# Scaling the attention products of a pair of heads: one vector product in place of two activations

## Chip, core and metric

The kernel runs on one core of a Trainium2 chip. The metric is the device time of one execution in microseconds; the median of the runs of a kernel counts.

## What is computed

Two layers of a hybrid backbone on 256 context and 512 latent tokens of width 1024. Each layer has modulated normalisation, one input projection, three groups of heads side by side (differential attention, grouped-query attention, a bidirectional gated delta rule), an output projection, and a SwiGLU. What matters here is the attention of the first two groups:

```python
# differential: 4 heads, two score components of 32 columns each, V of 64 columns
s = jnp.einsum('bqhcd,bkhcd->bhcqk', q, k).astype(jnp.float32) * scale
p = jax.nn.softmax(s, axis=-1)
p = p[:, :, 0] - lam * p[:, :, 1]
return jnp.einsum('bhqk,bkhe->bqhe', p.astype(v.dtype), v)
# grouped-query: 6 query heads, 2 key/value heads, 64 columns
s = jnp.einsum('bqhgd,bkhd->bhgqk', qg, k).astype(jnp.float32) * dh ** -0.5
p = jax.nn.softmax(s, axis=-1)
o = jnp.einsum('bhgqk,bkhd->bqhgd', p.astype(v.dtype), v)
```

Latent queries read all 768 tokens, context queries the 256 context tokens. Context outputs are computed in the first layer alone.

## The kernel before

The ten attention heads are worked off as five pairs of heads: two pairs of differential heads (numbers 0 and 1) and three pairs of grouped-query heads (2 to 4), in the order of `HORD`. For each pair, `attention` (line 1270) calls `attend` (line 1175) once per block of 128 queries: six blocks in layer 0, four in layer 1. That makes 30 and 20 calls, 50 in all. The letters of `ASTEP` (line 51) say at which step of a pair the next block of queries runs (`a`), the next pair's operands are loaded and turned (`f`, `t`), the pair before is finished (`o`), and control goes back to the surrounding plan (`y`).

One call does the following for both heads of the pair. `scores` (line 1166) multiplies queries and keys into a PSUM tile of two banks; there are two such tiles, used in turn. `softmax` (line 1156) takes the row maximum from it on VectorE (line 1162, tile `nm`), and ScalarE writes the exponentials `P` to SBUF, with their row sums in a column of `Z` (line 1163). A grouped-query head has one component, a differential head two; for the latter, VectorE forms the factor `cR` and adds the second component to the first (lines 1188 to 1191). The reciprocal `R` of the first sum is taken for each head as soon as its softmax is written (line 1186). The unnormalised `P` is then turned by TensorE, up to three blocks of 128 columns into one PSUM bank (`pt`, line 1197), and copied to `PT` in SBUF; by `EVD` (line 47), the first of the copies of a head with one component goes to VectorE (line 1199), the others to ScalarE (line 1201). Over the kernel that is 140 softmaxes and 180 copies, 60 of them on VectorE.

After both heads come the products with V: both heads side by side into the first 128 columns of one bank (`pv`, line 1207), a copy `OTs` on ScalarE (line 1209), and a transpose into columns 128 to 255 of the same bank (line 1210). Two activations then write the 64 columns of each head to `O`, scaled by that head's `R` (lines 1211 and 1212). `O` holds the outputs of a pair for all tokens; `attn_post` (line 1237) normalises those of differential heads, turns them and passes them on.

`pt`, `pv` and the transposes of operands (`exp`, `stk`) share one ring of PSUM banks (`ring`, line 150). It has two banks, `m0` and `m1`; from the step `w0` of the plan on there are four. A bank is free again when its last reader is through. `R` and `Z` each have four buffers.

In between, the plan (`PLAN`, line 38) sets the steps of the gated delta rule (`gdn_invert`, `gdn_post`, `gdn_step`, `gdn_out`), whose matmuls, copies and vector work stand in the same queues. The plan sets the order in which work is written down; the order on each engine is then drawn up when the kernel is built, from priorities and a simulated timeline (line 1668: `schedule_with_timeline_sim=True`). The engines themselves work in order. In the profile, helpers stand for the lines that call them: L186 is any activation, L189 a copy on ScalarE, L165 a product or sum of two tensors, L183 a fused scalar and tensor operation, L192 a matmul, L195 a transpose.

Of the kernel before, what the change touches and what calls it, by code (L numbers as in the profile page):

```python
# [13 lines left out]
AF = mybir.ActivationFunctionType  # L14
ALU = mybir.AluOpType
# [64 lines left out]
class Region:  # L80
# [8 lines left out]
    def slot(self, name, dt=F32, tag="s"):  # L89
        return self.pool.tile([128, self.cols], dt, tag=tag, name=name, bufs=self.tags[tag])  # L90
# [8 lines left out]
class Net:  # L99
# [16 lines left out]
    def slot(self, name, dt=F32, tag="s"):  # L116
        return self.R.slot(name, dt, tag)

# [166 lines left out]

    def ada_rows(self, R):

        self.cb = []
        for i in range(2):
            b = R.tiny("cb", [128, 1024], bufs=2)  # L290
            self.dma(b, self.A["crow"][i:i + 1].to_broadcast([128, 1024]))
            w = self.W.slot("adaw", F32, "raw")
            self.act(w, b, AF.Tanh, scale=0.5)
            self.stt(b, w, 1.0, b, ALU.add, ALU.mult)
            self.cb.append(b)

    def ada_row(self, R, w, l, ct, src, queue):

        queue.dma_start(out=w, in_=src)
        m = self.md[l][:, ct]  # L300
        j = R.tiny("junk", [128, 1024], mybir.dt.bfloat16)
        for ci in range(2):
            self.stt(j, w, 0.5, self.cb[ci], ALU.mult, ALU.mult, accum_out=m[:, ci:ci + 1])
        self.add(m, m, self.adab[:, l, ct:ct + 1].to_broadcast([128, 2]), self.g)

    def ada_next(self):

        if self.ada_todo:
            l, ct = self.ada_todo.pop(0)
            self.ada_row(self.R, self.W.slot("adaw", F32, "raw"), l, ct, self.A["ada_t"][48 * l + ct], self.nc.scalar)  # L310

# [473 lines left out]
    def gdn_post(self, l, tt):  # L785
        Z = self.GP.slot("Z")
        self.g.memset(Z[:, :768], 0.0)
        Zv = Z[:, :768].rearrange("p (h i) -> p h i", i=64)
        w = BLK[l][[tt in g for g in GDN_GROUPS].index(True)]
# [6 lines left out]
        T = self.GP.slot("ZT")  # L796
        self.v.transpose(out=T[:, :768], in_=Z[:, :768])
        Tv = T[:, :768].rearrange("p (h i) -> p h i", i=64)
# [354 lines left out]
        self.dma(xv[:, t0:], src[:, t0:])  # L1153
        return xv

    def softmax(self, ps, nk, zi, Z):

        P = self.slot("P", tag="p")
        nm = self.tiny("nm", [128, 1], bufs=4)
        pin = ps[:, :, :384] if nk == 768 else ps  # L1160
        pout = P[:, :768].rearrange("p (a b) -> p a b", a=2) if nk == 768 else P[:, :nk]
        self.v.tensor_reduce(out=nm, in_=pin, axis=AX.XY if nk == 768 else AX.X, op=ALU.max, negate=True)  # L1162
        self.act(pout, pin, AF.Exp, bias=nm, accum_out=Z[:, zi:zi + 1])
        return P

    def scores(self, pairs, qt, nk):
# [8 lines left out]
    def attend(self, l, pair, O, qts):  # L1175

        for qt in qts:
            nk = TOK if qt >= 2 else CTX
            nkb = nk // 128
            PTs, Rs = [], []  # L1180
            for comps, V in pair:
                Z = self.tiny("Z", [128, 2], bufs=4)
                Ps = [self.softmax(self.scores(pr, qt, nk), nk, ci, Z) for ci, pr in enumerate(comps)]
                P = Ps[0]
                R = self.tiny("R", [128, 1], bufs=4)
                self.v.reciprocal(out=R, in_=Z[:, 0:1])
                if len(comps) == 2:
                    c = self.tiny("cR", [128, 1], bufs=4)
                    self.v.reciprocal(out=c, in_=Z[:, 1:2])
                    self.stt(c, c, self.lam[:, l:l + 1], Z[:, 0:1], ALU.mult, ALU.mult)  # L1190
                    self.stt(P[:, :nk], Ps[1][:, :nk], c, P[:, :nk], ALU.mult, ALU.add)
                PT = self.slot("PT", tag="q")
                for i, k0 in enumerate(range(0, nk, 384)):
                    n = min(384, nk - k0)
                    ps = self.ring("pt")
                    for k in range(0, n, 128):
                        self.tr(ps[:, k:k + 128], P[:, k0 + k:k0 + k + 128])
                    if i < EVD[l][len(comps) - 1]:
                        self.v.tensor_copy(PT[:, k0:k0 + n], ps[:, :n])
                    else:  # L1200
                        self.cp(PT[:, k0:k0 + n], ps[:, :n])
                PTs.append(PT)
                Rs.append(R)
            pv = self.ring("pv")
            for kb in range(nkb):
                for c in range(2):
                    self.mm(pv[64 * c:64 * c + 64, :128], pair[c][1][:, kb], PTs[c][:, 128 * kb:128 * kb + 128], kb == 0, kb == nkb - 1)
            OT = self.R.tiny("OTs", [128, 128], bufs=2)
            self.cp(OT, pv[:, :128])
            self.tr(pv[:, 128:256], OT)  # L1210
            for c in range(2):
                self.act(O[:, qt, 64 * c:64 * c + 64], pv[:, 128 + 64 * c:192 + 64 * c], AF.Identity, scale=Rs[c])

    def attn_prep(self, l, i):

# [457 lines left out]
```

## Time and profile before

| | |
|---|---|
| median of 3 runs | 2218.24 us (2215.98 to 2219.58) |
| profiled execution, own time | 2220.72 us |
| its span | 2218.9 us |
| mean granted clock of TensorE | 0.928 of full speed |
| instructions | 37524 |
| busy: TensorE, VectorE, ScalarE, GpSimd | 2038.1, 1371.7, 850.0, 494.0 us |

The table of busy time says how much of the span an engine works; a TensorE that is busy is not necessarily at its peak, since the ends of its matmuls are modelled. The lists of waits say which engine stood idle in front of a group of instructions, and whose instruction ended that; "issue" means that nothing in the profile shows a cause. PE is TensorE's matmul, PEld its weight load, DVE VectorE, ACT ScalarE, POOL GpSimd, SP SyncE.

### The profile page before, as it was taken

Reading aid. Unit: us, or ns where it says so; the run is one execution under the profiler, and the core shown is the slowest. Engines: PE = TensorE matmul, PEld = TensorE weight load, DVE = VectorE, ACT = ScalarE, POOL = GpSimd, SP = SyncE. Lnnn points to the kernel's source line nnn. Section 1 sums busy time; section 2 is a strip of 40 time slices with the busy share of each in tenths; the row PEclk is TensorE's granted clock in tenths of the full one; section 3 lists DMA queues with packets and bytes.
Section 4 is the critical chain, followed back from the end, with each engine's and each line's share of the span. In section 5 each row is a group of like instructions: output and inputs, shape, how many; then the busy total and the mean of one; then the engine's idle time right before and its main releaser. Section 6 shows DMA issues by size and latency. Waiting matters only on the chain. (4 is left out here: it accounts for less than half of the span.)

```text
span 2218.9 us, 37524 instructions
## 1 busy us (share of the span) xinstructions
PE 2038.1 (92%) x14786; PEld 1688.2 (76%) x14786; DVE 1371.7 (62%) x2565; ACT 850.0 (38%) x1709; POOL 494.0 (22%) x797
## 2 busy tenths in 40 slices
PE   7999968798889999999999899975898989999997
PEld 3777766575668888888888789764676688888887
DVE  6747865757645646665756576688658655444444
ACT  5434235556644321212122444222566644222223
POOL 2204487230004101000000420456212022000002
PEclk9999976797899999999999999996599999999999
DMA  8345443120152324343424312343211152322331
GB/s 297 132 158 166 147 121 79 46 66 19 40 208 82 108 85 161 106 132 100 157 95 138 130 58 66 114 128 103 53 44 53 47 184 92 108 76 98 103 104 58
DMA packets 167601, 236.51 MB, mean 107 GB/s; under 512 B 75328, under 2 KB 109248, under 8 KB 167424
## 3 DMA queue, kind: packets, MB, share of 16 engines
q10 hardware_dynamic: 46160, 144.92, 20.1%
q1 hardware_dynamic: 121264, 89.18, 13.2%
q8 instruction: 117, 1.92, 0.3%
q14 instruction: 60, 0.49, 0.1%
HBM read 198.00 MB, written 36.04 MB: 105 GB/s over the span
## 5 line engine op out<-in xcount | busy, mean ns | idle before, releaser
L189 ACT ACTIVATE whi<-raw 128x1024 fp32r<-128x1024 f32 (+4 forms) x246 | 220.9, 912 | 484.9 <-PE dps L192 196.3
L165 DVE TENSOR_TENSOR wlo<-raw,whi 128x1024 fp32r<-128x1024 f32 (+4 forms) x236 | 249.0, 1068 | 221.9 <-ACT whi L189 220.0
L192 PE MATMUL gu<-ahi,wlo 128*128 128x512 f32 x672 | 262.5, 391 | 1.1 <-DVE wlo L165 1.1
L192 PE MATMUL gu<-ahi,whi 128*128 128x512 f32 x672 | 262.2, 391 | 0.0
L192 PE MATMUL dps<-acth,whi 128*128 128x512 f32 (+1 forms) x560 | 184.3, 345 | 0.6 <-ACT acth L189 0.4
L192 PE MATMUL dps<-acth,wlo 128*128 128x512 f32 (+1 forms) x560 | 183.9, 344 | 0.0
L192 PE MATMUL gu<-alo,whi 128*128 128x512 f32 x672 | 167.0, 390 | 0.0
L183 DVE SCALAR_TENSOR_TENSOR junk<-adaw,cb 128x1024 bf16<-128x1024 f32 x112 | 136.9, 1222 | 37.2 <-DMA adaw<-ada_t 36.3
L1162 DVE TENSOR_REDUCE nm<-S 128x1 f32<-128x768 f32 (+1 forms) x140 | 117.5, 845 | 57.6 <-PE S L192 56.2
L192 PEld LDWEIGHTS gu<-ahi,wlo 128*128 128x128 f32 x672 | 126.2, 188 | 27.6 <-DVE wlo L165 1.5
L192 PE MATMUL tps<-whi,ahi 128*128 128x512 f32 (+4 forms) x368 | 136.7, 376 | 10.8 <-ACT gk L189 8.0
L192 PEld LDWEIGHTS gu<-alo,whi 128*128 128x128 f32 x672 | 126.1, 188 | 26.7
L192 PEld LDWEIGHTS gu<-ahi,whi 128*128 128x128 f32 x672 | 126.3, 188 | 25.7
L183 DVE SCALAR_TENSOR_TENSOR h<-dps,md,h 128x512 f32<-128x512 f32 (+1 forms) x128 | 80.5, 633 | 104.6 <-PE dps L192 104.4
L192 PE MATMUL tps<-wlo,ahi 128*128 128x512 f32 (+4 forms) x368 | 138.1, 376 | 2.5 <-DVE wlo L165 2.5
L192 PE MATMUL tps<-whi,alo 128*128 128x512 f32 (+4 forms) x368 | 136.4, 371 | 0.0
L165 POOL TENSOR_TENSOR sqc<-sqc 128x256 f32<-128x256 f32 x35 | 34.0, 971 | 448.2 <-ACT sqc L186 447.7
L186 ACT ACTIVATE P<-S,nm 128x768 f32<-128x768 f32 (+1 forms) x140 | 114.3, 817 | 48.8 <-DVE nm L1162 35.6
L165 POOL TENSOR_TENSOR md<-md,adab 128x2 f32<-128x2 f32 x56 | 33.0, 588 | 434.9 <-DVE junk L183 434.9
L192 PE MATMUL dps<-actl,whi 128*128 128x512 f32 (+1 forms) x560 | 123.0, 344 | 0.0
L192 PEld LDWEIGHTS dps<-acth,whi 128*128 128x128 f32 x560 | 105.2, 188 | 15.2 <-ACT acth L189 0.6
L192 PEld LDWEIGHTS dps<-acth,wlo 128*128 128x128 f32 x560 | 105.2, 188 | 14.5
(315 smaller groups left out, 4740.2 us busy)
## 6 DMA issues: line engine op xcount, KB each, us to landing
raw<-w_u ACTq DMA_DIRECT2D x88, 512.0 KB
adaw<-ada_t ACTq DMA_DIRECT2D x56, 512.0 KB
adaw<-ada_p ACTq DMA_DIRECT2D x24, 512.0 KB
raw<-w_o ACTq DMA_DIRECT2D x24, 512.0 KB
raw<-w_d ACTq DMA_DIRECT2D x44, 256.0 KB
raw<-w_d ACTq DMA_DIRECT2D x32, 320.0 KB
adaq<-ada_q SPq DMA_DIRECT2D x16, 512.0 KB
raw<-w_t ACTq DMA_DIRECT2D x16, 512.0 KB
```

Source lines behind the costliest of these rows:

```text
L165: (eng or self.v).tensor_tensor(out=out, in0=a, in1=b, op=op)
L183: self.v.scalar_tensor_tensor(out=out, in0=a, scalar=sc, in1=b, op0=op0, op1=op1, **k)
L186: self.s.activation(out=out, in_=in_, func=func, **k)
L189: self.s.activation(out=out, in_=in_, func=AF.Copy, **k)
L192: self.t.matmul(out, lhsT, rhs, start=start, stop=stop)
L1162: self.v.tensor_reduce(out=nm, in_=pin, axis=AX.XY if nk == 768 else AX.X, op=ALU.max, negate=True)
```

## The change

The row sums of both heads of a pair go into one tile `Z` of 2x2 columns. One reciprocal takes the first column of both heads, after the softmaxes, the combinations and the transposes of both are written. One product of two tensors on VectorE writes both heads' 64 columns to `O`, out of PSUM, with `R` spread over 64 columns each, in place of the two activations on ScalarE. `Z` and `R` keep four buffers each, now one per pair and not one per head.

```diff
-    def softmax(self, ps, nk, zi, Z):
+    def softmax(self, ps, nk, z):
...
-        self.act(pout, pin, AF.Exp, bias=nm, accum_out=Z[:, zi:zi + 1])
+        self.act(pout, pin, AF.Exp, bias=nm, accum_out=z)
...
-            PTs, Rs = [], []
-            for comps, V in pair:
-                Z = self.tiny("Z", [128, 2], bufs=4)
-                Ps = [self.softmax(self.scores(pr, qt, nk), nk, ci, Z) for ci, pr in enumerate(comps)]
+            PTs = []
+            Z = self.tiny("Z", [128, 2, 2], bufs=4)
+            for hd, (comps, V) in enumerate(pair):
+                Ps = [self.softmax(self.scores(pr, qt, nk), nk, Z[:, hd, ci:ci + 1]) for ci, pr in enumerate(comps)]
                 P = Ps[0]
-                R = self.tiny("R", [128, 1], bufs=4)
-                self.v.reciprocal(out=R, in_=Z[:, 0:1])
                 if len(comps) == 2:
                     c = self.tiny("cR", [128, 1], bufs=4)
-                    self.v.reciprocal(out=c, in_=Z[:, 1:2])
-                    self.stt(c, c, self.lam[:, l:l + 1], Z[:, 0:1], ALU.mult, ALU.mult)
+                    self.v.reciprocal(out=c, in_=Z[:, hd, 1:2])
+                    self.stt(c, c, self.lam[:, l:l + 1], Z[:, hd, 0:1], ALU.mult, ALU.mult)
                     self.stt(P[:, :nk], Ps[1][:, :nk], c, P[:, :nk], ALU.mult, ALU.add)
...
                 PTs.append(PT)
-                Rs.append(R)
+            R = self.tiny("R", [128, 2], bufs=4)
+            self.v.reciprocal(out=R, in_=Z[:, :, 0])
             pv = self.ring("pv")
...
             self.tr(pv[:, 128:256], OT)
-            for c in range(2):
-                self.act(O[:, qt, 64 * c:64 * c + 64], pv[:, 128 + 64 * c:192 + 64 * c], AF.Identity, scale=Rs[c])
+            self.mul(O[:, qt].rearrange("p (c d) -> p c d", c=2), pv[:, 128:256].rearrange("p (c d) -> p c d", c=2),
+                     R.unsqueeze(2).to_broadcast([128, 2, 64]))
```

## Rows read from the trace of the kernel before

**Rows 1.** The page: busy time of each engine, share of the span, instructions.
```profile
PE 2038.1 (92%) x14786; PEld 1688.2 (76%) x14786; DVE 1371.7 (62%) x2565; ACT 850.0 (38%) x1709; POOL 494.0 (22%) x797
```

**Rows 2.** Busy time by stretch, 340 to 660 plus 1560 to 1785 us.
```profile
sum 545.00, PE 476.12 PEld 358.07 DVE 346.56 ACT 326.44 POOL 105.94; mean PE 238.06 PEld 179.04 DVE 173.28 ACT 163.22 POOL 52.97
```

**Rows 3.** 1680 to 1720 us: engines' busy time, clock, DMA; then tile O on ACT.
```profile
1680.00:1720.00 40.00, 33.95 (x395) 26.73 (x391) 39.33 (x123) 25.97 (x62) 4.18 (x5) 0.88 0.13 38
...
1680.00:1720.00 40.00, 2.06 (x8) 0.88 0.13 38
```

**Rows 4.** Tile R: what its instructions waited for (us, times), whole span.
```profile
  PE pv L195: 20.7, 19
  ACT O L186: 5.1, 5
  ACT P L186: 5.0, 9
```

**Rows 5.** Groups of ACT, DVE: busy us, mean ns of one | idle before, releaser.
```profile
L186 ACT ACTIVATE O<-pv,R 128x64 f32<-128x64 f32 x100 | 25.9, 312 | 21.0 <-PE pv L195 20.7
...
L1162 DVE TENSOR_REDUCE nm<-S 128x1 f32<-128x768 f32 x112 | 106.2, 951 | 46.0 <-PE S L192 44.9
...
L1186 DVE RECIPROCAL R<-Z 128x1 f32<-128x1 f32 x100 | 14.6, 155 | 10.8 <-ACT O L186 5.1 <-ACT P L186 5.0
```

**Rows 6.** Timeline, 1739.8 to 1742.2 us: start, duration, instruction, idle before and releaser.
```profile
1741.17 0.27 PE L195 MATMUL pv<-ident,OTs 128*128 128x128 f32 x1
...
1741.37 0.96 DVE L1162 TENSOR_REDUCE nm<-S 128x1 f32<-128x768 f32 x1
1741.48 0.52 ACT L186 ACTIVATE O<-pv,R 128x64 f32<-128x64 f32 x2 [1.34 <-PE pv L195]
...
1742.05 0.33 PE L195 MATMUL pt<-ident,P 128*128 128x128 f32 x1 [0.28 <-ACT O L186]
```

**Rows 7.** PE's waits, 340 to 660 us: us in total, times, longest.
```profile
PE S L192 <- ACT P L186: 5.2, 10, 1.2
...
PE pv L192 <- ACT PT L189: 2.5, 5, 0.7
PE pt L195 <- ACT O L186: 2.4, 3, 1.6
...
PE exp L195 <- ACT O L186: 1.5, 2, 0.9
...
PE otr L195 <- ACT O L186: 0.6, 1, 0.6
```

**Rows 8.** The same for weight loads, 340 to 660 us.
```profile
PEld pt L195 <- ACT O L186: 4.2, 8, 1.8
...
PEld exp L195 <- ACT O L186: 1.9, 2, 1.1
...
PEld otr L195 <- ACT O L186: 0.8, 1, 0.8
```

**Rows 9.** Waits of PE and of its weight loads, 1560 to 1785 us.
```profile
PE S L192 <- ACT P L186: 5.6, 10, 1.9
...
PE pv L192 <- ACT PT L189: 2.4, 3, 1.4
...
PE pt L195 <- ACT O L186: 0.8, 3, 0.3
...
PEld pt L195 <- ACT O L186: 1.8, 4, 0.5
...
PEld exp L195 <- ACT O L186: 0.2, 1, 0.2
```

**Rows 10.** Products of gk (two rows) and of X on DVE: ns min/median/max, first and last start.
```profile
L165 DVE TENSOR_TENSOR gk<-gk,arskv x12: 279/280/1844, 241.0 to 1490.1; 128x128 f32<-128x128 f32 x12
L165 DVE TENSOR_TENSOR gk<-gk,arsgq x10: 547/553/560, 283.7 to 1531.8; 128x384 f32<-128x384 f32 x10
...
L165 DVE TENSOR_TENSOR X<-scan,U x44: 548/554/561, 342.2 to 1697.2; 64x384 f32<-64x384 f32 x44
```

**Rows 11.** All waits: ACT's exponentials for row maxima.
```profile
ACT P L186 <- DVE nm L1162: 35.6, 34, 4.5
```

## Prediction

> **What bounds the kernel now.** First the table of busy time: TensorE (PE) is busy 92% of the span, VectorE (DVE) 62%, ScalarE (ACT) 38% [rows 1]. The change touches attention only, so the next view is busy time by stretch. Attention runs in 340 to 660 us (layer 0) and 1560 to 1785 us (layer 1). In these 545 us PE is busy 476.1, which leaves 68.9 us idle; DVE is busy 346.6 and ACT 326.4, so 64% and 60% [rows 2]. The two helper engines are about equally loaded there: moving work from one to the other is not a move to a free engine. One stretch has another limit: from 1680 to 1720 us DVE is busy 39.3 of 40 us while ACT has 26.0, and four of the pairs of activations that the change removes lie in it [rows 3].
>
> Next, the removed work itself. The 100 activations into O take 312 ns each, 25.9 us together, and ACT stood idle 20.7 us in front of 19 of them for PE's transpose of the products [rows 4, 5]. A pair overlaps and takes 0.52 us from start to end [rows 6]. The same rows show the pattern to look for: the transpose at 1741.17, the pair at 1741.48, and PE's next transposes of P, which want a bank of PSUM, at 1742.05, idle 0.28 us with ACT's O named as releaser. While `rings` holds two banks, `pv` keeps one of them until both activations are through.
>
> Last, PE's list of waits, since only PE's idle time in these stretches is to be had. O ended 9 waits of PE's matmuls, 5.3 us together, and 16 of its weight loads, 8.9 us [rows 7 to 9]. Other work of ACT ended more: P in front of new scores 10.8 us in 20 waits, the copies PT in front of the product with V 4.9 us in 8 [rows 7, 9].
>
> **The change part by part.** *Removed from ACT:* 50 pairs at 0.52 us, 25.9 us of busy time, and their 20.7 us of idle time. *Added to DVE:* 50 products of 128x128 out of PSUM with a factor spread over 64 columns. The trace has the same shape and spread out of SBUF: gk<-gk,arskv, median 280 ns, at worst 1844. What PSUM adds I take from two products with 384 columns: 553 ns out of SBUF, 554 out of PSUM, so nothing [rows 10]. I take 0.29 us. *Reciprocals:* 100 of one column at 155 ns become 50 of two columns [rows 5]; I leave the price at 0.155 us, and a second column at double price would add 7.8 us of DVE time, hidden like the rest. DVE's balance per pair is 0.29 - 0.155 = +0.135 us, 6.8 us over 50.
>
> *On the path, the bank.* From the end of the transpose to the release of `pv`, 0.52 us become 0.29, if DVE is as free as ACT was: 0.23 us less. I count the 16 places where O ended a wait of PE's weight loads: 16 x 0.23 = -3.7 us. Ends: nothing, if each of these waits is taken over by another; and if each product stands behind a row maximum (951 ns, [rows 5]), 16 x (0.95 - 0.23) = +11.5 us. I take the first value, as the busy shares of 64% and 60% give both engines nearly the same chance of being occupied.
>
> The Trainium skill's page "Perfetto Trace Analysis", section "Optimizing Scalar/DVE Operations", speaks against this step: it puts the overhead of one operation on PSUM at some 125 ns for VectorE and 51 for ScalarE. An estimate from that page, with the clocks of 0.96 and 1.2 GHz that its page "Trainium Kernel Development and Optimization", section "NeuronCore Architecture", gives, puts 128 columns at 0.26 us and twice 64 at 0.21, and the term would be about +0.8 us in place of -3.7. The rows above disagree with it on both sides: no surcharge for PSUM on DVE, and 0.52 us for the pair.
>
> *On the path, ACT's queue.* What stands behind a removed pair comes 0.52 us sooner. ACT has 140 exponentials P and, by the code, 120 of the 180 copies PT (60 go to DVE); about one in five of these 260 has a pair right in front of it (50/260 = 0.19). Of the 28 waits of PE that P and PT ended, that makes 28 x 0.19 x 0.52 = -2.8 us. Ends: nothing, where P itself was late because its row maximum was (P waited 35.6 us for it in 34 places, [rows 11]); and all 28 shortened by a whole pair, -14.6 us.
>
> *On the path, DVE.* Where PE or ACT sets the pace, 0.135 us more on DVE are hidden under PE's matmuls; if that cover is gone everywhere they cost 6.8 us. They surely count where DVE is saturated: four pairs, 4 x 0.135 = +0.5 us. DVE also loses waits: its reciprocal R stood idle 10.8 us, 5.0 for P's sum and 5.1 for an older pair of O that still read R's buffer [rows 4, 5]. The new reciprocal is written after both heads, when the sums have long been there, and four buffers now hold four pairs of heads, not two. In its place the product itself waits for PE's transpose, on DVE, with row maxima behind it; that is the rival below. I enter both at nothing.
>
> *Buffers and DMAs:* Z and R grow to 16 and 8 bytes a row; no transfer is issued, moved or put behind a wait; SP's and POOL's queues stay as they are. The square and the transposes of O after each head group now wait for DVE, 0.23 us sooner or a row maximum later, four and fifty times; both lie inside the bounds above. The order on each engine is drawn up at build time, so neighbours may trade places anywhere in attention; the trace of before can't price that, and the bounds of the two path terms are my measure of it.
>
> Sum: -3.7 - 2.8 + 0.5 = **-6.0 us**. The profiled execution took 2220.72 us, 2.5 above the median of 2218.24, with a span of 2218.9; the removed work is the same in both, so the median becomes about 2212. About 0.2%, 4.4 us, is what a measurement of this kernel can tell from no change.
>
> **The rivals.** *Slower: DVE waits where ACT waited.* DVE works in order. If the product stands there before the transpose is done, the 20.7 us that ACT lost come to DVE, and the next row maximum is late, with it P and the scores behind it. For it: P already waits for row maxima in 34 places [rows 11], and from 1680 to 1720 us DVE has nothing to spare. Against it: 10.8 us of idle time at the reciprocals leave the same queue. Price: 20.7 - 10.8 + 6.8 (all of DVE's extra work then counts) = +16.7, less 2.8 for ACT's relief: +13.9 us, 2232. It decides once idle time in front of the product passes some 7 us (10.8 + 2.8 - 6.8). The same page and section of the Trainium skill advises moving work to ScalarE when VectorE is saturated, which is this change turned round; rows 3 bear that out for 40 of the 545 us.
>
> *No change: PE's next wait takes over.* A release that comes sooner only lets PE reach the next transposes, which need P, or scores, which need a bank that P still holds. For it: P and its row maximum end more of PE's waits than O does. Against it: 5.3 us of waits are O's alone. Time: 2218, give or take 4.
>
> *Far faster: ACT was the brake.* If all 28 waits that P and PT end shrink by a whole pair: -3.7 - 14.6 + 0.5 = -17.8 us, 2200. For it: ACT feeds both of PE's commonest waits. Against it: only one in five has a pair in front.
>
> *Not what it says:* the 50 products would have to take as long as the pairs, 0.5 us, as some of arskv's did beside POOL's work (its longest was 1844 ns). Then the bank term vanishes and the balance is about -2 us; it falls in the case of no change.
>
> **How the numbers follow.** Forecast (-12 to -1 us around -6): chance 0.48, of it 0.33 beyond 4.4 us and 0.15 within. Far faster: 0.10. No change: 0.17, of it 0.14 within 4.4 us, 0.01 above and 0.02 below. Slower: 0.25. So faster 0.33 + 0.10 + 0.02 = 0.45, same 0.15 + 0.14 = 0.29, slower 0.25 + 0.01 = 0.26. The range reaches to the far faster case, 2200, and into most of the slower one, 2230; beyond the ends lie half of the first and some of the second, under 2 in 10. The forecast's own range is 2206 to 2217.
>
> **What would show it.** Right: 50 products at 0.28 to 0.30 us; 50 reciprocals at about 0.155 with little idle time in front; waits of PE for the product below 5.3 us; ACT's busy time down by about 26 us; waits of scores for P below 10.8 us. Wrong: idle time in front of the product well over 7 us with row maxima behind it, P's waits for them above 35.6 us, attention's two stretches longer than 545 us; or a difference that lies outside attention, where nothing was changed.

## The result and the profile after

The changed kernel takes 2203.77 us (median of 4 runs, 2200.47 to 2204.93), the kernel before 2218.91 in the same session: ratio 0.993 [0.9909, 0.9951], 15.1 us less. Its profiled execution took 2204.24 us with a span of 2202.4, 16.5 less than the span before.

The change did to its own instructions what it says. The view of tile R shows duration (ns, min/median/max), first and last start, then idle time of the engine before them, by what ended it (us, times):

```profile
L1202 DVE RECIPROCAL R<-Z x50: 144/158/167, 357.8 to 1754.0; 128x2 f32<-128x2 f32 x50
L165 DVE TENSOR_TENSOR O<-pv,R x50: 268/280/292, 370.0 to 1767.1; 128x128 f32<-128x128 f32 x50
...
  ACT P L186: 18.0, 15
  PE pv L195: 9.3, 8
```

The product takes 280 ns, the reciprocal of two columns 158: both as priced. The idle time is not as forecast: 18.0 us in front of the reciprocal (10.8 before, [rows 5]) and 9.3 in front of the product. The table of busy time, to be read against [rows 1], has ACT 22.9 us lower and DVE 4.3 higher:

```profile
PE 2027.9 (92%) x14786; PEld 1679.3 (76%) x14786; DVE 1376.0 (62%) x2565; ACT 827.1 (38%) x1609; POOL 493.2 (22%) x797
```

PE is 10.2 us less busy with the same 14786 matmuls. The same matmuls took less time, and the granted clock, shown further down, goes with that. First, though, the waits on which the forecast rested. PE and its weight loads in attention of layer 0 (340 to 650 us; us in total, times, longest):

```profile
PE S L192 <- ACT P L186: 14.0, 13, 2.2
...
PE pv L192 <- ACT PT L189: 4.4, 6, 1.5
...
PEld exp L195 <- DVE O L165: 3.8, 3, 2.9
...
PE exp L195 <- DVE O L165: 3.2, 2, 2.8
...
PEld pt L195 <- DVE O L165: 1.4, 5, 0.6
...
PEld otr L195 <- DVE O L165: 0.9, 1, 0.9
...
PE otr L195 <- DVE O L165: 0.7, 1, 0.7
...
PE pt L195 <- DVE O L165: 0.4, 1, 0.4
```

and in layer 1 (1545 to 1770 us):

```profile
PE S L192 <- ACT P L186: 4.9, 9, 1.4
...
PEld pt L195 <- DVE O L165: 3.4, 4, 1.1
...
PE pt L195 <- DVE O L165: 2.5, 3, 0.9
...
PE pv L192 <- ACT PT L189: 0.5, 1, 0.5
...
PEld exp L195 <- DVE O L165: 0.2, 1, 0.2
```

P's own waits for row maxima, over the whole span, to be read against [rows 11]:

```profile
ACT P L186 <- DVE nm L1162: 44.7, 39, 4.6
```

Against [rows 7, 9]: matmuls wait 3.2 + 0.7 + 0.4 + 2.5 = 6.8 us for O, where it was 5.3; scores wait 14.0 + 4.9 = 18.9 us for P, where it was 10.8. Neither wait that I meant to shorten became shorter, and the kernel is 15 us faster all the same. Busy time by whole stage shows where. The kernel before: attention of layer 0, what lies between it and attention of layer 1 (two rows), attention of layer 1, the last SwiGLU (columns: window, its length, busy time and instructions of PE, PEld, DVE, ACT, POOL, granted clock, share of the DMA engines, GB/s):

```profile
352.00:706.00 354.00, 305.61 (x3010) 235.51 (x3010) 216.60 (x503) 194.44 (x479) 74.65 (x97) 0.86 0.24 73
706.00:1273.00 567.00, 560.43 (x3246) 493.98 (x3245) 355.71 (x568) 142.41 (x227) 71.54 (x108) 1.00 0.38 122
1273.00:1567.00 294.00, 244.71 (x1863) 208.62 (x1862) 219.79 (x434) 99.82 (x194) 119.81 (x204) 0.85 0.34 96
1567.00:1785.00 218.00, 195.76 (x2313) 149.20 (x2312) 144.50 (x336) 139.96 (x337) 34.19 (x40) 0.86 0.19 53
...
1862.00:2218.00 356.00, 344.56 (x1603) 286.44 (x1601) 156.59 (x217) 102.51 (x151) 15.89 (x29) 0.99 0.28 94
```

The changed kernel, the same stages between the same landmarks (first scores, first matmul of the SwiGLU, and so on; the first stage thus also holds what stands between the last scores and the SwiGLU):

```profile
347.00:693.00 346.00, 298.26 (x3005) 229.90 (x3005) 217.44 (x502) 180.90 (x418) 72.93 (x97) 0.88 0.24 74
693.00:1260.00 567.00, 560.28 (x3248) 493.93 (x3247) 355.58 (x569) 141.67 (x226) 70.75 (x108) 1.00 0.38 122
1260.00:1553.00 293.00, 247.29 (x1865) 211.32 (x1865) 222.03 (x435) 100.38 (x195) 120.98 (x204) 0.85 0.33 97
1553.00:1768.00 215.00, 192.90 (x2313) 145.45 (x2312) 146.85 (x336) 131.02 (x297) 33.85 (x40) 0.88 0.19 54
```

By these rounded windows, attention of layer 0 is 8 us shorter (7.3 by the first scores and the first matmul of the SwiGLU to a tenth), that of layer 1 3 us, and the first scores come 5 us sooner, at 347 instead of 352, ahead of any attention. In layer 0 PE's idle time hardly moved (354 - 305.6 = 48.4 us, then 346 - 298.3 = 47.7); its busy time fell by 7.3 us while the granted clock rose from 0.86 to 0.88. Time lost to the clock, (1 - clock) x window, falls from 49.6 to 41.5 us there, about as much as the stage got shorter (the clock is given in two digits, which leaves each figure open by some 2 us). On this account the saving in this stage is time that TensorE no longer spends at the lower of its two levels, 1.2 in place of 2.4 GHz; what is cause there and what effect, the account does not say. Over the span, length times mean clock is 2218.9 x 0.928 = 2059 before and 2202.4 x 0.934 = 2057 after.

When the clock falls can be seen at the start of attention, in the kernel before:

```profile
372.00:392.00 20.00, 18.42 (x268) 14.01 (x264) 17.49 (x32) 13.05 (x33) 6.21 (x7) 0.93 0.25 62
392.00:412.00 20.00, 13.44 (x101) 10.11 (x100) 17.31 (x64) 13.53 (x37) 5.25 (x5) 0.73 0.08 20
412.00:432.00 20.00, 16.88 (x307) 13.10 (x305) 10.70 (x26) 11.02 (x32) 7.36 (x10) 0.83 0.38 87
...
452.00:472.00 20.00, 19.14 (x371) 15.18 (x370) 7.78 (x18) 12.61 (x33) 4.88 (x6) 1.00 0.23 68
...
1560.00:1580.00 20.00, 20.00 (x211) 13.88 (x210) 8.98 (x16) 9.64 (x21) 3.26 (x4) 0.50 0.24 56
```

The fall to 0.73 comes with gaps in PE's work (13.4 of 20 us busy); the full grant is back where PE works almost without a gap (19.1 of 20). The busy share alone does not tell the grant, though: the last row, from the start of layer 1's attention, has PE busy all 20 us at a grant of 0.50.

What could have set PE's gaps anew? The instructions on the engines stand in another order: compared row by row in the built programs (one row for a run of like instructions, buffer numbers left out), 1084 of TensorE's 7853 rows differ, and 20 of SyncE's 291. (Such counts serve to compare kernels with each other; they depend on how the two lists are laid side by side, and the closest fit leaves some 300 of TensorE's.) The change replaces rows on DVE and ACT alone; the rest is the builder's, which draws the order from a simulated timeline that the change disturbed.

### The profile page after: what moved, and what is told of

Its sections match the earlier page's. It is cut to its first block, busy times and chain, and to the rows that moved or that the text cites. A ratio compares the mean times of both kernels' runs of the same rounds, so it can differ in the third digit from the quotient of the medians.

```text
span 2202.4 us, 37369 instructions
## 1 busy us (share of the span) xinstructions
PE 2027.9 (92%) x14786; PEld 1679.3 (76%) x14786; DVE 1376.0 (62%) x2565; ACT 827.1 (38%) x1609; POOL 493.2 (22%) x797
## 5 line engine op out<-in xcount | busy, mean ns | idle before, releaser
L186 ACT ACTIVATE P<-S,nm 128x768 f32<-128x768 f32 (+1 forms) x140 | 113.9, 814 | 56.9 <-DVE nm L1162 44.7
L192 PEld LDWEIGHTS dps<-acth,wlo 128*128 128x128 f32 x560 | 105.2, 188 | 14.4
```

What stands on the lines that cost most here:

```text
L186: self.s.activation(out=out, in_=in_, func=func, **k)
L192: self.t.matmul(out, lhsT, rhs, start=start, stop=stop)
```

## The experiments

Two theories to start with. *The part theory:* the gain comes from the product, the merged reciprocal, or from the buffers that reach four pairs instead of two. *The order theory:* any small change makes the builder draw another order, and the order sets the time. All ratios are against the kernel before in the same session; the edits of e1 and e2 are shown against the changed kernel.

**e1: reciprocal merged, activations kept.**

```diff
-            self.mul(O[:, qt]..., pv[:, 128:256]..., R.unsqueeze(2).to_broadcast([128, 2, 64]))
+            for c in range(2):
+                self.act(O[:, qt, 64 * c:64 * c + 64], pv[:, 128 + 64 * c:192 + 64 * c], AF.Identity, scale=R[:, c:c + 1])
```

> One part alone: Z per pair and one reciprocal of two columns, placed after both heads; the two activations stay on ScalarE. If the gain of some 15 us comes from ScalarE's relief (the 50 pairs gone), this kernel stays within 3 us of before, ratio 0.999 to 1.001. If it comes from the reciprocals (50 fewer on VectorE, 10.8 us of idle time in front of them), it is 4 to 8 us faster, ratio 0.996 to 0.998. If a newly drawn order on the engines is what counts, it moves by 5 us or more either way.

Measured: 2210.54 us (12 runs), ratio 0.997 [0.9955, 0.9984], 7.4 us less. That fits the reciprocals (4 to 8 us) and a newly drawn order (5 us or more) alike.

**e2: the product, with one reciprocal per head at its old place.**

```diff
+            R = self.tiny("R", [128, 2], bufs=4)
             for hd, (comps, V) in enumerate(pair):
...
                 P = Ps[0]
+                self.v.reciprocal(out=R[:, hd:hd + 1], in_=Z[:, hd, 0:1])
...
-            R = self.tiny("R", [128, 2], bufs=4)
-            self.v.reciprocal(out=R, in_=Z[:, :, 0])
```

> The other part alone: the product of two tensors on VectorE in place of the pair of activations, but a reciprocal of one column per head where it stood before (both into one tile). If ScalarE's relief is the cause, this kernel keeps nearly all of the gain, 12 to 17 us, ratio 0.992 to 0.995; VectorE has 50 reciprocals more than in the change, which costs at most 50 x 0.155 = 7.8 us. If the merged reciprocal is the cause, it stays within 4 us of before. If the newly drawn order counts, it lies anywhere between -20 and +5 us.

Measured: 2203.38 us (6 runs), ratio 0.9933 [0.991, 0.9956]. The whole gain without the merged reciprocal; e1 has somewhat less than half of it without the product. Read alone, this would credit the product with the rest.

**e3: the kernel before again.** No edit.

> The kernel before once more, for a second profile. In the two profiles at hand the first scores stand at 351.6 us before and 346.6 us after the change, though all work up to there is the same in both. If those 5 us belong to the execution and not to the change, this profile has its first scores up to 5 us away from 351.6; if they belong to the change, it has them within 1 us of 351.6.

Measured: 2218.89 us (one run), span 2217.1, clock 0.926. First scores at 349.7 us, 1.9 sooner than in the profile before, and everything after keeps that distance to 1 us. The start of the kernel moves by some us from one execution to the next (346.6 to 354.5 over all runs here); the 5 us of the changed kernel's start are within that.

**e4: the kernel before with eight buffers for Z and R.** Nothing else changed; activations and reciprocals as before.

```diff
-                Z = self.tiny("Z", [128, 2], bufs=4)
+                Z = self.tiny("Z", [128, 2], bufs=8)
...
-                R = self.tiny("R", [128, 1], bufs=4)
+                R = self.tiny("R", [128, 1], bufs=8)
```

> The kernel before with eight buffers of Z and of R in place of four, which is as many pairs deep as in the change; nothing else. If the deeper buffers matter, VectorE's 5.1 us of idle time in front of R for older pairs of O go and the kernel is 1 to 5 us faster, ratio 0.998 to 0.9995. If not, it is within 2 us of before. If a newly drawn order alone moves the time, it is more than 5 us away either way.

Measured: 2204.8 us (9 runs, 2200.78 to 2213.2), ratio 0.9946 [0.9929, 0.9962]. Nearly the whole gain without the product and without a merged reciprocal. Either depth matters, or the order: 930 of TensorE's rows differ from the kernel before.

**e5: the change, Z and R two pairs deep**, as deep as before.

```diff
-            Z = self.tiny("Z", [128, 2, 2], bufs=4)
+            Z = self.tiny("Z", [128, 2, 2], bufs=2)
...
-            R = self.tiny("R", [128, 2], bufs=4)
+            R = self.tiny("R", [128, 2], bufs=2)
```

> The change with two buffers of Z and of R in place of four, so that the reciprocal may run two pairs of heads ahead, as before the change, and not four. With e4_buffers this makes a square: activations or product, two or four pairs deep. If depth is the cause of the whole gain, this kernel is within 4 us of before, ratio 0.998 to 1.001. If the product is, it keeps 11 us or more, ratio below 0.995. If what counts is which order the planner draws, the square need not add up, and the time lies anywhere from -20 to +5 us.

Measured: 2215.5 us (12 runs), ratio 0.9989 [0.9974, 1.0003]: hardly a gain. Up to here most fits depth as the cause; e1, as deep as the changed kernel, has only half its gain.

**e6: the kernel before with R five deep, not four.** One buffer more, and an order almost untouched: 2 of TensorE's rows and 78 of VectorE's differ, none of ScalarE's.

```diff
-                R = self.tiny("R", [128, 1], bufs=4)
+                R = self.tiny("R", [128, 1], bufs=5)
```

> The kernel before with five buffers of R in place of four. TensorE's order has 2 of 7853 rows changed, ScalarE's none; on VectorE 78 rows, nearly all reciprocals R that now stand earlier. So nearly all of the wait for an older pair (5.1 us in front of R) goes without a newly drawn order. If waits for R's buffer cost time on the chip, it gains 4 to 13 us as e4_buffers did. If e4_buffers gained by its order (930 rows of TensorE changed), this kernel is within 3 us of before, ratio 0.9985 to 1.0015.

Measured: 2225.52 us (10 runs), ratio 1.0033 [1.0017, 1.0049]. Slower by 6.4 us, which neither theory held. Nor did the wait go: R still stands idle 5.1 us in 5 places for O, as in [rows 4], so this run does not tell what that wait costs. The trace puts the loss at the end: up to the first matmul of the last SwiGLU the run lies 1.2 us from the kernel before, and from there to the end it takes 363.2 us (2226.5 - 1863.3) in place of 356.8 (2218.9 - 1862.1), with the same matmuls in the same order at a clock of 0.99, as before. e5 has this too (2217.8 - 1855.2 = 362.6). That is a second effect, taken up in e9.

**e7: the kernel before with one useless copy**, of 128x64 on VectorE, in one of the 50 calls. No buffer, reciprocal or activation is touched.

```diff
             self.cp(OT, pv[:, :128])
+            if l == 0 and qts[0] == 3 and len(pair[0][0]) == 2 and not hasattr(self, "nud"):
+                self.nud = self.tiny("nudge", [128, 64])
+                self.v.tensor_copy(self.nud, OT[:, :64])
```

> The kernel before with one copy more: in a single one of the 50 calls, VectorE copies 64 columns of OTs to a tile that nobody reads. It costs 0.1 to 0.3 us. The planner answers with a new order behind it (592 of TensorE's 7853 rows changed). If the drawn order is what moved e4_buffers and the change, this kernel moves by 4 us or more, most likely down by 5 to 15 us. If the buffers or the product are the cause, it stays within 2 us of before, ratio 0.999 to 1.001.

Measured: 2202.87 us (6 runs), ratio 0.994 [0.9922, 0.9958]. An instruction more, with no use, gives 16 us, the change's whole gain. Its order differs from the kernel before in 592 rows of TensorE. Its stages, first attention of layer 0, then the stretch ahead of layer 1's attention, then that attention:

```profile
349.00:692.00 343.00, 300.48 (x3009) 231.54 (x3009) 214.79 (x502) 194.14 (x478) 74.28 (x97) 0.87 0.25 75
...
1259.00:1548.00 289.00, 238.54 (x1857) 206.10 (x1856) 217.48 (x433) 98.76 (x192) 122.96 (x204) 0.87 0.34 98
1548.00:1767.00 219.00, 194.08 (x2321) 147.10 (x2320) 146.39 (x337) 141.34 (x339) 33.16 (x40) 0.87 0.18 53
```

Here it is layer 0 (343 for 354 us) and the stretch from 1259 to 1548 (289 for 294) that are shorter, at ACT's full load of 194 us, and layer 1's attention isn't. Over the span, length times clock is 2201.7 x 0.934 = 2056 again. In layer 0 only about half of the gain goes with the clock: (1 - clock) x window falls from 49.6 to 44.6 us, and PE's idle time from 48.4 to 42.5, where the change had left it alone. So what the product takes off ACT is not needed for a gain of this size, and the same 16 us can come out of other stages.

**e8: the change with one useless copy** of one column, in one call.

```diff
                 P = Ps[0]
+                if l == 0 and qts[0] == 4 and pair[0][0].__len__() == 2 and not hasattr(self, "nud"):
+                    self.nud = self.tiny("nudge", [128, 1])
+                    self.v.tensor_copy(self.nud, Z[:, hd, 0:1])
```

> The changed kernel with one copy more: in a single call VectorE copies one column of Z to a tile that nobody reads, some 0.15 us. The planner draws a new order (895 of TensorE's 7837 rows changed against the change). If the product's gain is its own, whatever the order, the time stays within 3 us of the changed kernel, ratio to before 0.9915 to 0.9945. If the order sets it, it moves by 4 us or more from the changed kernel, either way.

Measured: 2202.88 us (6 runs, 2199.49 to 2207.16), ratio 0.9938 [0.992, 0.9956]: nothing by the median, which taken alone speaks for a gain that is the product's own. But the run is 26.2 us ahead of the kernel before when the last SwiGLU begins (1835.9 for 1862.1) and then loses 6.4 of it: that SwiGLU again takes 363.2 us.

What do e5, e6 and e8 share? The small tiles lie in front of the large ones in SBUF. By the built programs, the base of the large tiles is off that of the kernel before by -128, +32 and +32 bytes per partition in these three, and by 0 (the changed kernel, e1, e2) or +256 (e4, e7) where the SwiGLU takes its 357 us.

**e9: Z eight deep, for the place alone.** The order on every engine is row for row that of the kernel before; the large tiles lie 128 bytes further up.

```diff
-                Z = self.tiny("Z", [128, 2], bufs=4)
+                Z = self.tiny("Z", [128, 2], bufs=8)
```

> The kernel before with eight buffers for Z in place of four: the order on every engine stays row for row that of the kernel before, and all the large tiles behind the small pool move up by 128 bytes per partition. Three kernels so far (R five deep; the change two pairs deep; the change with a useless copy) need 6.2 us more for the last FFN (some 363 us instead of 356.8, same matmul order, clock 1.00), and in these three the large tiles' base is off the others' by an amount that is not a multiple of 256 bytes (+32, -128, +32; +0 or +256 in the others). Theory of the place in memory: the last FFN takes about 363 us here too, time about 2225 us, ratio 1.0028. Rival, the longer FFN belongs to the order drawn: nothing changes, 2219 us, ratio 1.000, FFN 356.8.

Measured: 2223.09 us (12 runs), ratio 1.0016 [1.0, 1.0032]. By the medians 3.3 us of the 6 expected; the traces are clearer. One group of the last SwiGLU's matmuls, in the kernel before:

```profile
L192 PE MATMUL gu<-ahi,wlo x320: 388/392/394, 1862.4 to 2178.7; 128*128 128x512 f32 x160
```

and in e9, where that stage begins at the same 1862.4 us:

```profile
L192 PE MATMUL gu<-ahi,wlo x320: 393/398/398, 1862.4 to 2184.8; 128*128 128x512 f32 x160
```

The median matmul takes 398 ns and not 392, and the last starts 6.1 us later. The span is 5.8 us longer, of it 5.8 in the last SwiGLU. The rival (that the longer SwiGLU belongs to an order) falls, as the order is the same.

**e10: e8 with the copy's tile 64 columns wide**, the copy still of one column: the order of e8 row for row, the large tiles at +256 bytes.

```diff
-                    self.nud = self.tiny("nudge", [128, 1])
-                    self.v.tensor_copy(self.nud, Z[:, hd, 0:1])
+                    self.nud = self.tiny("nudge", [128, 64])
+                    self.v.tensor_copy(self.nud[:, 0:1], Z[:, hd, 0:1])
```

> The change with the same useless one-column copy as before, into a tile of 64 columns, not one: same order on every engine, large tiles at +256 bytes from those of the kernel before in place of +32. Theory of the place in memory: the last FFN is back at about 356.8 us, and the time falls from 2202.9 to about 2196.5 us, ratio 0.990, faster than the change itself. Rival, the longer FFN belongs to this order: 2203 us again, ratio 0.994.

Measured: 2196.75 us (6 runs, 2194.29 to 2198.71), ratio 0.9901 [0.9884, 0.9917]: 6.1 us less than e8, and every run below the lowest of the changed kernel. This is the fastest of all here. It beats e8 by the placement, and the changed kernel, whose tiles are as well placed, in an order that a useless copy drew. Its matmuls are back at the shorter pitch, first in the view of that group, then by stage (layer 0's and layer 1's attention, the last SwiGLU):

```profile
L192 PE MATMUL gu<-ahi,wlo x320: 388/392/394, 1838.2 to 2154.5; 128*128 128x512 f32 x160
```

```profile
350.00:691.00 341.00, 295.17 (x3006) 227.28 (x3006) 216.87 (x501) 180.61 (x418) 73.90 (x97) 0.89 0.25 75
...
1547.00:1761.00 214.00, 191.44 (x2367) 145.10 (x2368) 147.38 (x337) 132.03 (x299) 34.68 (x40) 0.91 0.19 55
...
1838.00:2194.00 356.00, 344.55 (x1602) 286.42 (x1600) 156.43 (x217) 102.30 (x151) 15.91 (x29) 0.99 0.29 94
```

**e11: e5 with Z six deep**, so that the large tiles lie as in the kernel before; R stays two pairs deep, and the order is that of e5 row for row.

```diff
-            Z = self.tiny("Z", [128, 2, 2], bufs=2)
+            Z = self.tiny("Z", [128, 2, 2], bufs=6)
```

> The change with R two pairs deep as before, and Z six deep so that the large tiles lie where the kernel before has them: the order is that of the run with both two deep. Theory of the place in memory: last FFN 356.8 us in place of 363, time 2209 us, ratio 0.9957; then the product in the depth of the kernel before is worth about 10 us in the order it draws. Rival: 2215.5 us again, ratio 0.9989.

Measured: 2213.52 us (12 runs), ratio 0.9974 [0.9958, 0.999]. The last SwiGLU is back at 356.8 us (2208.7 - 1851.9), but the median fell by 2 us and not by 6, and the intervals of e5 and e11 overlap: by the medians this pair is inconclusive. The product at the old depth gains 6 us here. Tile R in this run:

```profile
L165 DVE TENSOR_TENSOR O<-pv,R x50: 252/281/293, 372.4 to 1774.8; 128x128 f32<-128x128 f32 x50
its engine sat idle before it (us, times) until:
  PE pv L195: 7.3, 8
  ACT P L186: 5.0, 9
```

Its reciprocal waits 5.0 us where the changed kernel's waits 18.0, and its product 7.3 for 9.3; yet it is the slower of the two by some 10 us. Less idle time there did not make this kernel the faster one.

**e12: the kernel before with three buffers for R**, one less; Z five deep keeps the large tiles in place. The order differs in 579 rows of TensorE from the kernel before and in only 49 from e7.

```diff
-                Z = self.tiny("Z", [128, 2], bufs=4)
+                Z = self.tiny("Z", [128, 2], bufs=5)
...
-                R = self.tiny("R", [128, 1], bufs=4)
+                R = self.tiny("R", [128, 1], bufs=3)
```

> The kernel before with three buffers for the reciprocal in place of four, and five for Z so that the large tiles lie where they did. The order is redrawn: 579 rows of TensorE differ from the kernel before, only 49 from that of the neutral copy that took 2202.9 us. Theory that the order drawn sets the time: close to that run, 2203 us (2198 to 2210), ratio 0.993, though it has a buffer less. Rival, that gains come from buffers that let VectorE and ScalarE run ahead (as eight of them seemed to, 2204.8): a buffer less is no faster than before, 2219 us or more, ratio 1.000 or above.

Measured: 2207.06 us (6 runs), ratio 0.9943 [0.9923, 0.9962], with ACT at its full load of activations. One buffer less for R is nearly as good as four more, and about as good as e7, whose order it nearly has. R waits longer here for older pairs of O than in the kernel before (5.1 us in 5 places, [rows 4]):

```profile
  ACT O L186: 8.6, 9
```

Yet the kernel is 12.7 us faster. The depth theory falls with this; the fifth buffer of Z is no way out, since eight of them gain nothing in e9.

**What the runs leave.** Not one of the change's three parts is needed for a gain of this size: e7 and e12 have 16 and 13 us with none of them. What they share with the changed kernel is a newly drawn order. How much of the change's own 15 us is the order's is not shown: what the product itself is worth stays open, since no run changes it in an unchanged order; taking it out always redraws. Runs with well-placed tiles give, with activations, 2218.9, 2210.5, 2204.8, 2202.9 and 2207.1 (before, e1, e4, e7, e12), a mean of 2208.8; with the product, 2203.8, 2203.4, 2196.8 and 2213.5 (after, e2, e10, e11), a mean of 2204.4. The difference of 4 us is about my forecast's size, but orders alone spread over 16 us, so nine draws don't show it. Span times mean clock, averaged over all runs of a kernel, is 2058 to 2064 with the product and 2053 to 2060 with activations: nothing there says that the product spares TensorE any work.

## Why the prediction was right, and where it was not

The time after, 2203.77 us, lies in the range of 2200 to 2230, and faster was the likeliest sign. The mechanism was wrong all the same: 15.1 us came where 6.0 were forecast, and neither of the two gains in the sum can be found in the trace. That the time fell into the range is luck. It lies near the end that the range had for the far faster rival, with ACT as the brake; but scores waited longer for P, not less, and e7 and e12 are as fast, or nearly, with ACT's full load.

- *Prices of the parts: right.* 280 ns for the product (0.29 taken), 158 for the reciprocal (155 taken). ACT lost 22.9 us of busy time, near the 26 expected, and DVE gained 4.3 (6.8 expected). No surcharge shows for PSUM on DVE: 280 ns out of it, 280 for gk out of SBUF [rows 10]. The Trainium skill's page "Perfetto Trace Analysis", section "Optimizing Scalar/DVE Operations", gives VectorE an overhead of about 60 ns on SBUF and 125 on PSUM; no such difference between the two is seen in these runs. The estimate of 0.26 us that the prediction made from that page for the product is near the 0.28 measured; it is the pair that the estimate had too short, 0.21 for 0.52.
- *The bank, -3.7 us: not seen.* I said that waits for the product below 5.3 us would bear it out. They are 6.8 us for matmuls, and for weight loads 3.8 + 1.4 + 0.9 in layer 0 and 3.4 + 0.2 in layer 1, 9.7 in place of 8.9.
- *ACT's queue, -2.8 us: not seen.* Scores wait 18.9 us for P, not less than 10.8. Waits of the product with V for PT stay at 4.9 us (4.4 + 0.5).
- *DVE's idle time: wrong.* I held that R's new place leaves "little idle time in front", as the sums "have long been there". It is 18.0 us; in the order that was drawn the reciprocal stands close behind the last exponential. In e11's order it is 5.0, in e10's 14.4.
- *The slower rival* would decide, I wrote, once idle time in front of the product passes 7 us. It is 9.3 us, and P's waits for row maxima, the second sign that I had named for it, rose from 35.6 us [rows 11] to 44.7. The kernel is faster: the condition was met and the price was not paid. Idle time in front of the product and the total time don't go together in e11 and e10 either (7.3 us at 2213.5, 4.7 at 2196.8).
- *The step that failed* is "the trace of before can't price that, and the bounds of the two path terms are my measure of it", said of neighbours that trade places when the order is drawn up. Those bounds were local: so many waits, each longer or shorter by one instruction. In place of that, the runs show an order redrawn over the whole of attention, and with it less time lost at the lower clock: about 8 us in layer 0 (49.6 to 41.5), and 218 x 0.14 - 215 x 0.12 = 4.7 us in layer 1. That moved gaps link the two is likely and not shown. e7 shows the size of the term: 16 us for an instruction that does nothing. It should have stood in the sum as its largest uncertainty, with nothing on its side but a spread.
- *The other queues: wrong in part.* I held that no transfer is moved and SP's queue stays as it is; 20 of SyncE's 291 rows stand elsewhere.
- *The test I named for being wrong*, a difference outside attention, is met in part: of the profile's 16.5 us, 5 lie ahead of attention, within the spread of the start over all profiles; and in e7 5 us come out of the stretch ahead of layer 1's attention, which its edit doesn't touch.

## What to carry to other kernels

Where a builder draws the order, a change of a few instructions is compared through two drawn orders: before crediting the change, draw the old kernel's order anew with a neutral copy or one buffer more or less, and see how far the time moves. Check from the built programs how many rows of the order differ, and where the large tiles lie. If neutral draws spread as widely as the gain, then say that the order is what was found, and take the best one as a separate step.

## What the runs showed of the hardware

- **Span times granted clock hardly moves.** In the ten profiles with well-placed tiles the span times the mean granted clock stays within 2052 to 2063 (before 2059, after 2057, e7 2056, e10 2061) with no trend, while spans run from 2194.7 to 2218.9. In layer 0's attention the grant is 0.86 in the kernel before and 0.89 in e10. Within a stage it need not hold: layer 0's attention in e7 has 343 x 0.87 = 298, for 354 x 0.86 = 304 before. Whether an order is better because its gaps are kinder to the clock, or its gaps are smaller because the clock was higher, these runs can't separate.
- **The place of tiles in SBUF moves the pitch of matmuls.** Shifted by 128 bytes per partition, in the same order on every engine, the last SwiGLU's 128x512 matmuls take 398 ns, not 392, and the stage 362.6 us, not 356.8 (e9). All 13 kernels here fit one rule: 357 us at shifts of 0 and +256 bytes, 363 at -128, +32 and +128. At +32 the stage's three groups of these matmuls have a median of 394 ns each (e6, e8), at 128 either way 393, 398 and 396 (e5, e9). Whether it is the distance of 256 that counts, and which of the tiles has to lie so (activations and weights all move together), was not tried. The transfers don't explain it: over the stage's first 290 us their queue is busy 30.2% for 28.84 MB in the kernel before (1.05% a MB), 30.1% for 27.84 MB in e9 (1.08%), but 31.1% for 28.84 MB in e4 (1.08% too), where the stage is short. The Trainium skill's page "DMA: Bandwidth & Descriptors", section "How a descriptor splits into AXI transactions", has a boundary of 256 bytes for transfers; no run here ties it to the pitch. In layer 0 the group gu<-alo,whi takes a mean of 389 ns in either place.
- **The start varies.** Over the 14 profiles first scores come between 346.6 and 354.5 us, without any attention ahead of them; single profiles can't be compared to better than that.
